# Five small reorderings in a hybrid mLSTM and windowed-attention layer: softmax negation, factor stores, key tanhs, side stores, and the loads of a scan

## The chip, the cores and the metric

The kernel runs on one core of a Trainium2 chip. The metric is the device time of one execution in microseconds, and the median of several runs is compared. A core has a tensor engine (PE), a vector engine (VectorE, DVE in the profile), a scalar engine (ScalarE, ACT), GpSimd (POOL) and SyncE (SP), which here does nothing but issue DMAs. Each engine takes its own list of instructions in order. Tiles move between HBM and SBUF by DMA; PE writes to PSUM banks, which VectorE and ScalarE empty.

## The reference

One layer over a sequence of 4096 rows of width 1024. A norm and an input projection give the columns of two groups of heads. Group A is a matrix memory (mLSTM), scanned in 32 chunks of 128 rows, once in each direction:

```
qk_a = jax.nn.silu(centred_depthwise_conv(qk_a, conv_w, conv_b))
h = sigmoid(o_a) * (h_fwd + h_bwd)
y_a = rms(h) * mhn_w * silu(z_a)
```

In each chunk the scan has scores of q and k times a decay matrix E, a part from the carried state C times the weighted q (W), a division by the larger of two denominators, and the update of the state. Group B is attention in a window of 128 rows to either side, with 8 query heads of 64 on 2 key heads, a position bias and a sink logit:

```
m = jnp.maximum(jnp.max(scores, axis=-1), sink_l)
p = jnp.exp(scores - m[..., None])
denom = jnp.sum(p, axis=-1) + jnp.exp(sink_l - m)
```

Both outputs are concatenated and go through an output projection; the input is added, and a last norm ends it. All of it is fp32, and matrices are split into a high and a low part so that three products give fp32 accuracy.

## The kernel before, in words

Four stages follow one another. `pass1` (L161) reads x in 16 blocks of 256 rows, norms and transposes it, projects queries, keys and values of group B and does the attention. `pass2` (L876) goes backwards over 8 blocks of 512 rows, makes q, k and v of group A with the convolution, and carries the backward state. `pass3` (L1411) does the scans of both directions in 32 chunks, and beside them a stream of gate projections (`gate_stream`, L1268) with seven products P0 to P6 in place of eight for each pair of chunks. `tail` is the output projection and the last norm.

The order of PE's work is written out by hand: `interleave` and `place` set pieces of one kind of work between units of another at given fractions. The instructions of the other engines are put in order by a scheduler, from the order in which the program issues them and their dependences; `behind(c, ins)` says that what is issued inside it may stand no earlier than `ins`, and `high_priority` draws PSUM evictions ahead. Tiles come from pools that are used in turn: a load into a tile waits until the last reader of the buffer's former tile is done. Two of them matter here: `xtile` (14 buffers of 4 KB per partition, for E, W, CC, the raw rows r and the operands op) and `slot` (2 KB tiles, for hs, z, o and others).

*Attention.* A slot is a key head of a chunk of 128 queries, 64 in all. `att_a` (L361) does a slot's scores in four groups g: two matmuls into `sp` (L379), then one VectorE instruction (L382) that adds the bias, writes the negated scores `s` and leaves their minimum with the negated sink in a column of `NG`. After the fourth group come four exponentials on ACT (L390), each of which uses one column of `NG`, so that each may run as soon as its own column is there. `att_t` transposes (L410; copies to `pt`, L412 on ACT and L413 on VectorE), `att_o` multiplies by v (L424; evictions to `ab`, L436 and L437) and stores `at_d` (L439). In slot sl the scores are those of slot sl+2.

*The last attention stretch* (from about 500 us) has 16 pieces `w2_piece`, each of which loads a part of the value weights (`w2s`, L575) and scales and splits it (L696 on ACT, L697 on VectorE). `keep_first` (L612) stores the norm factors of the first rows, six DMAs of 128 single words to `rs_d` (L615), and is the piece hooked in at place 8.

*pass2.* `qkproj(b, m)` makes one projection of 512 columns of block b: 24 matmuls `up` (L1031), the copy U (L1035), the convolution of one ACT step (L1048) and four VectorE steps (L1050), and then `finish` (L1052): tanh on ACT (L1054), a product on VectorE (L1055), a store. m 0 to 3 are queries, 4 to 7 keys; the tanh of m = 7, and in all blocks but the last also of 0 and 3, is put off by `c.late`. `ktp` (L1092) transposes a key head and splits it to `kt` (L1098, L1099), `kvmm` (L1115) updates the state C (L1134) and stores `kf_d` (L1140). `side(b)` (L983) fits in loads, sums and stores that prepare the gate products.

*pass3.* `load_scan` (L1241) issues the loads of a chunk by name: q, k, kf, v, CC (the backward state) and, in two broadcast halves each, E and W. In chunk n the loop at L1537 loads CC, E and W of chunk n+2, makes the forward state (`state`, L1453) of chunk n+1 with kf, and loads kf of n+2; then its pieces among 42 matmuls of the gate stream: `decays` of n+1 (masks of E on POOL, L1437, exponentials on ACT, L1441), four `heads` (L1465), the load of v for n+2 with `weigh_q` (L1459, W times q) of n+1, `yout` (L1508, transposes `yp` and a store) of n−1, `scores` (L1444, S and its product with E) of n+1, and last `FIN` (L1503: hs times its norm times z; the norm's power is done on POOL, L1499). In the gate stream `ahead(i)` (L1342), which is called four matmuls into product i, splits the operand of product i+1 (ACT copy L1288, subtraction L1289 on VectorE or POOL) and issues the loads that a small plan lists: whole operands 5 and 6 and the next pair's 0, and raw rows 3 and 2. `evict` (L1310) empties a product with additions to o and z.

## Time and profile before

| what | value |
|---|---|
| median of 3 runs | 2195.59 us (2193.04 to 2196.16) |
| the profiled execution | 2192.97 us, of which its span is 2191.2 us |
| PE busy | 2126.5 us, 97% |
| VectorE, ACT, POOL busy | 1544.2, 1139.0, 710.6 us |
| granted clock of PE | 0.997 |
| HBM read, written | 305.20 MB, 153.17 MB |

Durations and waits are those of the one profiled execution. A row of the trace in order of time has the start in us from the span's start, the time in us, the engine, the line, the operation, the tiles (out<-in), the shape, a count where neighbours are merged, and in brackets how long the engine had stood idle and what released it. SPq is SyncE's queue of DMA issues. A row of waits has the total in us, how many times, and the longest. The stages lie at about 0 to 600 us (`pass1`), 600 to 1200 (`pass2`), 1200 to 1715 (`pass3`) and from there to the end (`tail`).

### The profile page before, as it was taken

To read this page: it belongs to the slowest core of one execution; us is meant where nothing else is said; L and a number is where in the kernel's file an instruction comes from. 1 tells how busy PE (TensorE), PEld (TensorE's weight loads), DVE (VectorE), ACT (ScalarE), POOL (GpSimd) and SP (SyncE) were. 2 spreads that over 40 slices of the span, in tenths; PEclk is the share of its full clock that TensorE was granted. 3 is DMA by queue.
4 is the path that set the end of the run, shared out by engine and by line. 5 is a ranking of instruction groups with operands and counts; after the bars stand their busy time and mean duration, and the time that the engine had idled before them with its cause. 6 is when DMAs were issued, how large, how long until landed. Compare 5 with 4: busy or idle time off the path is not lost.

```text
span 2191.2 us, 35245 instructions
## 1 busy us (share of the span) xinstructions
PE 2126.5 (97%) x12034; PEld 1839.1 (84%) x12034; DVE 1544.2 (70%) x3195; ACT 1139.0 (52%) x2764; POOL 710.6 (32%) x1049
## 2 busy tenths in 40 slices
PE   8999999998999999999999999999999999999998
PEld 7999999998898787888887888888887788888886
DVE  6677777777877777677647777776667543877776
ACT  7788888876653444444434554555455321333323
POOL 3576665651013333332311322323222111112222
PEclk9999999999999999999999999999999999999999
DMA  7665654543236745654586988777878998667765
GB/s 255 188 207 149 186 190 139 185 133 82 71 118 228 238 160 170 236 188 132 170 274 239 305 278 264 247 242 258 271 252 291 334 355 286 184 186 185 192 191 146
DMA packets 286433, 460.72 MB, mean 210 GB/s; under 512 B 23851, under 2 KB 151851, under 8 KB 284716
## 3 DMA queue, kind: packets, MB, share of 16 engines
q1 hardware_dynamic: 246880, 323.94, 45.2%
q0 software_dynamic: 39136, 134.25, 20.5%
q8 instruction: 95, 1.56, 0.3%
q14 instruction: 86, 0.70, 0.1%
q10 hardware_dynamic: 236, 0.27, 0.0%
HBM read 305.20 MB, written 153.17 MB: 209 GB/s over the span
## 4 chain that ended last, share of the span: by engine, by line
PE 60%; DMA 14%; DVE 10%; issue 7%; ACT 5%; POOL 3%; SPq 1%; POOLq 0%; ACTq 0%; DVEq 0%
PE up L1031 13%; PE qp L547 8%; PE P L1337 6%; PE v2p L1004 6%; DMA xr<-x 5%; PE op L424 3%; PE tp L410 3%; DMA E<-m_d 3%; PE sp L379 3%; PE zbp L151 3%; PE zbp L153 3%; PE zbp L152 3%; DMA xb<-xT_d 2%; DMA W<-w_d 2%; PE num L1474 1%
## 5 line engine op out<-in xcount | busy, mean ns | idle before, releaser
L1337 PE MATMUL P<-wt,op 128*128 128x512 f32 x1344 | 365.7, 407 | 14.0 <-DVE z L1325 11.6
L1031 PE MATMUL up<-xb,w 128*128 128x512 f32 x1344 | 334.7, 396 | 0.0
L1685 PE MATMUL o<-wo,yo 128*128 128x512 f32 (+1 forms) x1356 | 312.3, 392 | 0.0
L1685 PEld LDWEIGHTS o<-wo,yo 128*128 128x128 f32 x1356 | 253.3, 188 | 59.0
L1337 PEld LDWEIGHTS P<-wt,op 128*128 128x128 f32 x1344 | 237.5, 189 | 62.0 <-DVE z L1325 15.4
L1031 PEld LDWEIGHTS up<-xb,w 128*128 128x128 f32 x1344 | 245.0, 188 | 48.8
L1050 DVE SCALAR_TENSOR_TENSOR qk<-U,cw,qk 128x512 f32<-128x512 f32 x256 | 197.3, 771 | 85.3 <-ACT qk L1048 73.5
L547 PE MATMUL qp<-xT,wqb 128*128 128x256 f32 x1536 | 242.6, 288 | 0.1
L547 PEld LDWEIGHTS qp<-xT,wqb 128*128 128x128 f32 x1536 | 214.4, 190 | 8.5 <-DVE wqb L320 0.5
L413 DVE TENSOR_TENSOR pt<-tp,pt 128x512 fp32r<-128x512 f32 x188 | 129.6, 690 | 68.6 <-ACT pt L412 66.7
L390 ACT ACTIVATE s<-s,NG 128x320 f32<-128x320 f32 (+1 forms) x256 | 142.3, 557 | 50.8 <-DVE NG L382 49.3
L382 DVE CUSTOM_DVE_ANT_0 s<-sp,G,nsink 128x320 f32<-128x320 f32 (+1 forms) x256 | 138.0, 539 | 38.6 <-PE sp L379 36.7
L1004 PE MATMUL v2p<-w,xb 128*128 128x512 f32 x672 | 158.3, 395 | 2.9 <-DMA xb<-xT_d 2.2
L1004 PEld LDWEIGHTS v2p<-w,xb 128*128 128x128 f32 x672 | 125.8, 188 | 34.1 <-DMA xb<-xT_d 3.5
L412 ACT CAST pt<-tp 128x512 fp32r<-128x512 f32 x188 | 109.9, 584 | 46.7 <-PE tp L410 21.7
L424 PE MATMUL op<-pt,v 128*128 128x512 f32 x376 | 122.0, 406 | 10.2 <-DVE ab L437 9.4
L1488 ACT ACTIVATE hs<-num,r 128x128 f32<-128x128 f32 x128 | 46.9, 366 | 157.2 <-DVE r L1485 90.6
L379 PE MATMUL sp<-kk,q 128*128 128x320 f32 (+2 forms) x512 | 119.5, 314 | 3.2 <-DVE NG L382 2.2
L410 PE MATMUL tp<-ident,s 128*128 128x128 f32 x752 | 113.0, 272 | 0.2 <-DVE pt L413 0.2
L151 PE MATMUL zbp<-xc,w 128*128 128x512 f32 x256 | 102.4, 400 | 2.6 <-DVE az L1400 1.4
L1503 DVE SCALAR_TENSOR_TENSOR hs<-hs,ss,z 128x128 f32<-128x128 f32 x128 | 46.5, 424 | 79.8 <-POOL ss L1499 79.8
L1054 ACT ACTIVATE th<-qk 128x512 f32<-128x512 f32 x64 | 40.5, 632 | 116.6 <-DVE qk L1050 116.6
(306 smaller groups left out, 4641.0 us busy)
## 6 DMA issues: line engine op xcount, KB each, us to landing
xc<-xT_d SPq DMA_DIRECT2D x64, 512.0 KB, 7.5
xT_d<-xT POOLq DMA_DIRECT2D x52, 512.0 KB, 6.4
xb<-xT_d SPq DMA_DIRECT2D x48, 514.0 KB, 8.6
op<-xT_d SPq DMA_DIRECT2D x96, 256.0 KB, 5.3
E<-m_d SPq DMA_DIRECT2D x64, 256.0 KB, 6.4
W<-w_d SPq DMA_DIRECT2D x64, 256.0 KB, 6.8
y<-y_d SPq DMA_DIRECT2D x32, 512.0 KB, 3.5
out<-xr POOLq DMA_DIRECT2D x31, 512.0 KB, 6.1
```

The costliest lines, as they stand in the source:

```text
L151: nc.tensor.matmul(out, wl, xh, start=first, stop=False)
L379: nc.tensor.matmul(sp[:, lo:hi], qt, kk[:, kv, z, col - 128 + lo:col - 128 + hi], start=(z == 0), stop=(z == 1))
L382: nc.vector.tensor_tensor_reduce(out=s[:, lo:hi], in0=sp[:, lo:hi], in1=bias[0][:, kv * 2 + m, lo - 64 * half:hi - 64 * half], op0=ALU.add ...
L390: LAST["act"] = nc.scalar.activation(ps[g][:, kept(g)], ps[g][:, kept(g)], AF.Exp, scale=-1.0, bias=ng[:, g:g + 1], accum_out=rs[:, g:g + 1])
L410: nc.tensor.transpose(tp[:, g * 128:(g + 1) * 128], ps[g][:, j * 128:(j + 1) * 128], c.ident)
L424: nc.tensor.matmul(op, vt, pt[:, z, :], start=(i == 0 and z == 0), stop=(i == len(js) - 1 and z == 1))
L547: nc.tensor.matmul(qp, wq[k // 2][:, k % 2, w, m * 128:m * 128 + 128], x[k], start=(k == 0 and j == 0), stop=(k == KT - 1 and j == 2))
L1004: nc.tensor.matmul(vp, a, wv[k // 2][:, k % 2, m, :], start=(k == 0 and j == 0), stop=(k == KT - 1 and j == 2))
L1031: nc.tensor.matmul(up[:, 0:hi - lo], w[k // 2][:, k % 2, a, cs], x, start=(k == 0 and j == 0), stop=(k == KT - 1 and j == 2))
L1050: nc.vector.scalar_tensor_tensor(acc, U[:, t:t + 512], cw[:, cm, t:t + 1], acc, ALU.mult, ALU.add)
L1337: nc.tensor.matmul(P[i], OPS[j, i][:, k, z, :], c.wt[i][k][m], start=k == 0 and a == 0, stop=k == 3 and a == 2)
L1685: nc.tensor.matmul(p, a[:, z, k, :], w[k // 2][:, k % 2, m, lo:hi], start=k == 0 and z == 1, stop=k == 3 and z == 0 and m == 0)
```

## The change

Five edits, all in the order of instructions but for the first:

1. *Softmax.* The VectorE instruction of a group now keeps the scores with their sign and leaves their maximum in a column of a new tile `st`; after the fourth group one further VectorE instruction on 128×4 elements negates the four maxima and takes the minimum with the negated sink, into `NG`. The four exponentials read `NG` and so all come behind it.
2. *Factor stores.* `keep_first` is hooked in at place 94 in place of 8, behind the last `w2_piece`.
3. *Key tanhs.* The tanh and product of all key projections m = 4 to 7 are put off; those of 4, 5 and 6 are issued behind the convolution of the projection that follows.
4. *Side stores.* What `side` issues from the second list stands behind the latest store of `kf_d`.
5. *Scans.* W and CC are loaded for chunk n+1 in chunk n (before: n+2); `state(n)` makes the state of n+1 in chunk n, behind the product of the scores with E; v is loaded at the piece before the third head and for n+1, kf of n+2 with the piece that had v; the operands 5, 6 and the next 0 are loaded one product later; `weigh_q(0)` goes behind the first product with E.

The diff:

```diff
@@ att_a
-                ST[sl] = ([], list(range(jl // 128, jr // 128)))
-            ps, _ = ST[sl]
+                st = wk.tile([128, 4], F32, tag="st", bufs=4, name=f"st{sl}")
+                ST[sl] = ([], list(range(jl // 128, jr // 128)), st)
+            ps, _, mx = ST[sl]
...
-                                           op0=ALU.add, op1=ALU.min, scale=-1.0,
-                                           scalar=nsink[:, kv, half, m:m + 1], accum_out=ng[:, g:g + 1])
+                                           op0=ALU.add, op1=ALU.max, scale=1.0, scalar=-3e38,
+                                           accum_out=mx[:, g:g + 1])
             ps.append(s)
             if g < 3:
                 return
+            nc.vector.scalar_tensor_tensor(ng, mx, -1.0, nsink[:, kv].rearrange("p h m -> p (h m)"), ALU.mult, ALU.min)
             for g in range(4):
-                LAST["act"] = nc.scalar.activation(ps[g][:, kept(g)], ps[g][:, kept(g)], AF.Exp, scale=-1.0,
-                                                   bias=ng[:, g:g + 1], accum_out=rs[:, g:g + 1])
+                LAST["act"] = nc.scalar.activation(ps[g][:, kept(g)], ps[g][:, kept(g)], AF.Exp, bias=ng[:, g:g + 1],
+                                                   accum_out=rs[:, g:g + 1])
@@ pass1
-        hooks.append((8, keep_first))
+        hooks.append((94, keep_first))
@@ side
-                        f()
+                        with behind(c, c.kfs):
+                            f()
@@ qkproj
-                if m == 7 or m in (0, 3) and b:
+                if m > 3 or m in (0, 3) and b:
                     c.late[m] = finish
@@ kvmm
-                nc.gpsimd.dma_start(c.kf_d[n], kf.rearrange("p h d -> p (h d)"))
+                c.kfs = nc.gpsimd.dma_start(c.kf_d[n], kf.rearrange("p h d -> p (h d)"))
@@ pass2, after the units of projection m
+                if m > 4:
+                    c.late[m - 1]()
@@ ahead
-            plan = [(2, whole, j, 5), (3, whole, j, 6), (4, whole, j + 1, 0), (4, raw, j + 1, 3), (5, raw, j + 1, 2)]
+            plan = [(3, whole, j, 5), (4, whole, j, 6), (5, whole, j + 1, 0), (4, raw, j + 1, 3), (5, raw, j + 1, 2)]
             if j == 0:
-                plan = [(3, whole, 0, 5), (4, whole, 1, 0), (4, raw, 1, 3), (5, raw, 1, 2)]
+                plan = plan[:1] + plan[2:]
@@ pass3
         decays(0)
-        weigh_q(0)
...
         with behind(c, c.em):
-            state(0)
+            weigh_q(0)
             weigh_q(1)
...
             m = n + 1
+            if n:
+                load(m, ("w", "cc"))
+            if m < NCH:
+                with behind(c, c.em):
+                    state(n)
             with behind(c, c.rawd if n == 0 else None):
-                load(n + 2, ("cc", "e", "w"))
+                load(n + 2, ("e",))
                 if n == 0:
                     load(2, ("q",))
-            if n + 2 < NCH:
-                state(m)
-            with behind(c, c.rawd if n == 0 else None):
-                load(n + 2, ("kf",))
...
-            pieces.append(lambda: (load(n + 2, ("v",)), weigh_q(m) if m > 1 else None))
+            pieces.insert(4, lambda: load(m, ("v",)) if n else None)
+            pieces.append(lambda: (load(n + 2, ("kf",)), weigh_q(m) if m > 1 else None))
```

The rows below are places in an engine's order, with the program's names (a row has the line, the operation, out<-in and the shape; the last number of a name only tells instances apart). The lines of the changed kernel are two to six higher.

SyncE's order in the last attention stretch, where w2s00 to w2s07 and w2s10 to w2s17 are the sixteen parts of the value weights, at_d the attention's stores and v_d those of the values. Before:

```order
L575 DMA w2s01_6768<-w_in 128x512
L439 DMA at_d_70<-ab25_6710 128x512
L575 DMA w2s02_6830<-w_in 128x512
L615 DMA rs_d_79<-rstd0_0_164 128x1
L615 DMA rs_d_79<-rstd0_1_171 128x1
L615 DMA rs_d_79<-rstd1_292 128x1 x2
L615 DMA rs_d_79<-rstd2_521 128x1 x2
L575 DMA w2s03_6907<-w_in 128x512
```

and now:

```order
L577 DMA w2s16_7765<-w_in 128x512
L577 DMA w2s17_7807<-w_in 128x512
L606 DMA v_d_77<-v2t31_7607 128x516
L441 DMA at_d_70<-ab29_7739 128x512
L617 DMA rs_d_79<-rstd0_0_164 128x1
L617 DMA rs_d_79<-rstd0_1_171 128x1
L617 DMA rs_d_79<-rstd1_292 128x1 x2
L617 DMA rs_d_79<-rstd2_521 128x1 x2
L606 DMA v_d_77<-v2t29_7839 128x516
L441 DMA at_d_70<-ab30_7910 128x512
```

The six stores of rs_d stood between the parts w2s02 and w2s03 and now stand behind the last part, between two stores of the attention.

VectorE's order in block 6 of `pass2`, where qk6_7 is the fourth key projection and qk6_0 the one issued next, th the tanh, kt the transposed keys and C27 a state. Before:

```order
L1099 TENSOR_TENSOR kt6_1_1_9113<-ktp6_1_9107,kt6_1_0_9112 128x512
L1050 SCALAR_TENSOR_TENSOR qk6_7_9067<-U6_7_9038,cw_7335,qk6_7_9067 128x512 x2
L1055 SCALAR_TENSOR_TENSOR qk6_7_9067<-th6_7_9117,qk6_7_9067 128x512
L1134 SCALAR_TENSOR_TENSOR C27_9166<-C28_8652,decay_8180,kv27_0_9168 128x129
L1050 SCALAR_TENSOR_TENSOR qk6_0_9131<-U6_0_9080,cw_7335,qk6_0_9131 128x512
L1099 TENSOR_TENSOR kt6_2_1_9149<-ktp6_2_9143,kt6_2_0_9148 128x512
L1134 SCALAR_TENSOR_TENSOR C27_9166<-C28_8652,decay_8180,kv27_1_9177 128x129
```

and now:

```order
L1053 SCALAR_TENSOR_TENSOR qk6_7_9191<-U6_7_9162,cw_7445,qk6_7_9191 128x512 x2
L1102 TENSOR_TENSOR kt6_1_1_9241<-ktp6_1_9235,kt6_1_0_9240 128x512
L1058 SCALAR_TENSOR_TENSOR qk6_7_9191<-th6_7_9245,qk6_7_9191 128x512
L1053 SCALAR_TENSOR_TENSOR qk6_0_9259<-U6_0_9208,cw_7445,qk6_0_9259 128x512
L1102 TENSOR_TENSOR kt6_2_1_9277<-ktp6_2_9271,kt6_2_0_9276 128x512
L1053 SCALAR_TENSOR_TENSOR qk6_0_9259<-U6_0_9208,cw_7445,qk6_0_9259 128x512
L1137 SCALAR_TENSOR_TENSOR C27_9294<-C28_8780,decay_8304,kv27_0_9296 128x129
L1053 SCALAR_TENSOR_TENSOR qk6_0_9259<-U6_0_9208,cw_7445,qk6_0_9259 128x512
L1137 SCALAR_TENSOR_TENSOR C27_9294<-C28_8780,decay_8304,kv27_1_9305 128x129
```

The product with the tanh (L1055) came right behind the last steps of qk6_7, and now (L1058) the subtraction kt6_1_1 stands between them; kt6_2_1 stood behind the first update of C27 and now stands ahead of both. On ACT, the copy U and the first convolution step of the projections 5 to 7 now stand ahead of the tanh of the projection before.

SyncE's order in `pass3` for one pair of chunks: r are raw rows, op the operands of the gate products (op8_5 is the one of product 5 of pair 8), and the others the loads of a scan by chunk. Before:

```order
L1256 DMA lkf16_15914<-kf_d_76 128x516
L1234 DMA op8_5_16021<-xT_d_69 128x4x128 x2
L1256 DMA lv16_16012<-v_d_77 128x516
L1234 DMA op8_6_16065<-xT_d_69 128x4x128 x2
L1260 DMA CC17_16070<-cb_d_78 128x4x129
L1265 DMA E17_16072<-m_d_72 128x512
L1256 DMA lq17_16046<-q_d_74 128x512
L1265 DMA E17_16072<-m_d_72 128x512
L1256 DMA lk16_16044<-k_d_75 128x512
L1265 DMA W17_16075<-w_d_73 128x512 x2
L1256 DMA lkf17_16082<-kf_d_76 128x516
```

and now, for the next pair:

```order
L1270 DMA W17_16351<-w_d_73 128x512 x2
L1265 DMA CC17_16354<-cb_d_78 128x4x129
L1270 DMA E18_16360<-m_d_72 128x512
L1261 DMA lkf17_16304<-kf_d_76 128x516
L1270 DMA E18_16360<-m_d_72 128x512
L1261 DMA lq18_16335<-q_d_74 128x512
L1261 DMA lk17_16333<-k_d_75 128x512
L1239 DMA op9_5_16511<-xT_d_69 128x4x128 x2
L1261 DMA lv17_16417<-v_d_77 128x516
L1270 DMA W18_16516<-w_d_73 128x512 x2
L1265 DMA CC18_16519<-cb_d_78 128x4x129
L1270 DMA E19_16525<-m_d_72 128x512
```

E of a chunk now comes right behind W and CC of the chunk before it, W is loaded a chunk later than E, and op_5 stands ahead of one v and W in place of two chunks' loads.

VectorE's order from the product of the scores with E16 to hs15, where op9_4 is the subtraction that reads r9_3 last. Before:

```order
L1451 TENSOR_TENSOR E16_15904<-S16_16208,E16_15904 128x512 x2
L1489 SCALAR_TENSOR_TENSOR hs15_16131<-num15_2_16144,r15_1_16163,hs15_16131 128x128
L1493 SCALAR_TENSOR_TENSOR hs15_16131<-o15_15676,hs15_16131 128x512
L1328 TENSOR_TENSOR o17_16008<-P8_6_16204,o17_16008 128x512
L1289 TENSOR_TENSOR op9_2_16303<-r9_2_16181,op9_2_16303 128x4x128
L1463 TENSOR_TENSOR W18_16239<-W18_16239,lq18_16217 128x1024
L1498 TENSOR_SCALAR ss3_15_16172<-ss3_15_16172 128x4
L1503 SCALAR_TENSOR_TENSOR hs15_16131<-hs15_16131,ss3_15_16172,z15_15772 128x128 x4
```

and now:

```order
L1494 SCALAR_TENSOR_TENSOR hs15_16242<-num15_2_16266,r15_1_16283,hs15_16242 128x128
L1456 TENSOR_TENSOR E16_16028<-S16_16326,E16_16028 128x512
L1461 SCALAR_TENSOR_TENSOR CC17_16354<-CC16_16187,decay_8304,lkf16_16130 128x129 x4
L1294 TENSOR_TENSOR op9_4_16508<-r9_3_16235,op9_4_16508 128x4x128
L1498 SCALAR_TENSOR_TENSOR hs15_16242<-o15_15793,hs15_16242 128x512
L1333 TENSOR_TENSOR o17_16125<-P8_6_16321,o17_16125 128x512
L1503 TENSOR_SCALAR ss3_15_16292<-ss3_15_16292 128x4
L1488 SCALAR_TENSOR_TENSOR r16_0_16402<-num16_0_16388,TM_8490 128x4
L1489 TENSOR_TENSOR r16_0_16402<-r16_0_16402,num16_0_16388 128x4
L1490 RECIPROCAL r16_0_16402<-r16_0_16402 128x4
L1468 TENSOR_TENSOR W18_16516<-W18_16516,lq18_16335 128x1024
L1508 SCALAR_TENSOR_TENSOR hs15_16242<-hs15_16242,ss3_15_16292,z15_15884 128x128 x4
```

The subtraction op9_4 came behind hs15 and now stands ahead of it, the updates CC17 stand between the product with E16 and op9_4, and W18 stands ahead of hs15 in both.

More of the change, by code (lines that the diff above doesn't have):

```diff
@@ L403, in att_t @@
         def att_t(sl, i):
-            ps, js = ST[sl]
+            ps, js, _ = ST[sl]
             if i >= len(js):
```

## The prediction

> **What bounds the kernel now.** I read the page first, then TensorE's (PE's) waits by cause, then busy time by stage, and only then the instructions in order of time around the largest waits. The page's busy line and the costliest group:
>
> ```profile
> PE 2126.5 (97%) x12034; PEld 1839.1 (84%) x12034; DVE 1544.2 (70%) x3195; ACT 1139.0 (52%) x2764; POOL 710.6 (32%) x1049
> L1337 PE MATMUL P<-wt,op 128*128 128x512 f32 x1344 | 365.7, 407 | 14.0 <-DVE z L1325 11.6
> ```
>
> PE is busy 2126.5 of 2191.2 us. The change adds or removes no matmul, so nothing it does can be worth more than the 64.7 us in which PE stands still. Which of these it can reach is told by the waits of PE (total, times, longest):
>
> ```profile
> PE P L1337 <- DVE z L1325: 11.6, 12, 1.9
> PE op L424 <- DVE ab L437: 9.4, 10, 3.0
> PE ktp L1096 <- DVE kt L1099: 7.7, 5, 2.1
> PE sp L379 <- DVE NG L382: 2.2, 1, 2.2
> PE S L1449 <- DVE o L1328: 1.6, 1, 1.6
> ```
>
> and by the busy time of PE in stages (first time after the comma is PE; then PEld, DVE, ACT, POOL, clock, DMA share, GB/s):
>
> ```profile
> 100.00:500.00 400.00, 395.78 (x2986) 380.94 (x2985) 310.74 (x764) 323.62 (x844) 255.48 (x327) 1.00 0.55 168
> 500.00:600.00 100.00, 93.60 (x601) 84.13 (x600) 77.43 (x191) 67.31 (x167) 5.34 (x18) 0.97 0.25 67
> 1225.00:1700.00 475.00, 459.11 (x2661) 392.89 (x2660) 342.53 (x878) 251.34 (x784) 133.68 (x151) 1.00 0.81 264
> ```
>
> So attention's steady part leaves 4.2 us, its last stretch 6.4, the scans 15.9. Each edit touches one of these places. The clock is 0.97 to 1.00 in all of them and plays no part.
>
> **Factor stores.** SP's queue, and what stood behind it on ACT and PE:
>
> ```profile
> 506.24 2.81 SPq L615 DMA_DIRECT2D rs_d<-rstd  x6
> 509.15 12.46 SPq L575 DMA_DIRECT2D w2s<-w_in  x3
> DMA to landing us min/median/max: 2.7/2.9/9.4
> 519.76 1.37 ACT L696 ACTIVATE w<-w2s,nw 128x512 fp32r<-128x512 f32 x2 [5.21 <-DMA w2s<-w_in]
> 521.91 0.56 PE L379 MATMUL sp<-kk,q 128*128 128x320 f32 x2 [2.19 <-DVE NG L382]
> 526.86 1.22 PE L424 MATMUL op<-pt,v 128*128 128x512 f32 x2 [1.36 <-DVE ab L437]
> ```
>
> The third row is for the loads of w2s: 2.9 us as a rule, 9.4 at worst, and the worst is the one issued straight behind the six stores of single words. ACT takes its instructions in order, so it sat 5.21 us before the multiplication of that piece with softmax exponentials and PSUM copies queued behind it, and PE ran dry twice: 2.19 + 1.36 = 3.6 us. With the stores behind the last of the sixteen w2s loads nothing is queued behind them that PE waits for soon. I take −3.6, with ends −6.4 (all that PE idles from 500 to 600) and 0 (another load is late in its place).
>
> **Key tanhs.** Block 6, where the key projection's tanh is last:
>
> ```profile
> 718.97 0.63 ACT L1054 ACTIVATE th<-qk 128x512 f32<-128x512 f32 x1 [3.22 <-DVE qk L1050]
> 721.71 0.68 DVE L1099 TENSOR_TENSOR kt<-ktp,kt 128x512 fp32r<-128x512 f32 x1
> 722.54 0.63 PE L1096 MATMUL ktp<-ident,qk 128*128 128x128 f32 x4 [2.05 <-DVE kt L1099]
> ACT th L1054 <- DVE qk L1050: 116.6, 49, 3.3
> ```
>
> ACT reaches the tanh before the convolution's last VectorE step and stands 3.22 us; the next projection's copy U and the cast of kt stand behind it, VectorE gets its subtraction for kt at 721.71, and ktp6_3, which needs the PSUM bank that this subtraction reads, starts 2.05 us late. The wait on the tanh is paid 49 times, but only five of them reach PE, 7.7 us in all. In the new order ACT copies and begins the next projection ahead of the tanh of the one before, so VectorE goes from one projection to the next without that wait and comes to kt6_2_1 sooner, which also stands ahead of both updates of C27. The tanh of the last projection itself keeps its place on ACT, and its wait may stay. No instruction is added. Two of the five lie in block 0 (the largest at 1200.09, below), with other work around them than in block 6:
>
> ```profile
> 1200.09 0.63 PE L1096 MATMUL ktp<-ident,qk 128*128 128x128 f32 x4 [2.02 <-DVE kt L1099]
> ```
>
> Of these two I count half, so −6, with ends −7.7 and 0. The side stores that now follow kf_d on POOL delay writes that are read many tens of microseconds later: 0.
>
> **Scans.** A pair of chunks, in order of time:
>
> ```profile
> 1523.98 0.51 SPq L1265 DMA_DIRECT2D W<-w_d  x1
> 1524.59 0.43 SPq L1256 DMA_DIRECT2D lkf<-kf_d  x1
> 1533.60 1.21 SPq L1234 DMA_DIRECT2D op<-xT_d  x2
> 1537.49 0.56 SPq L1265 DMA_DIRECT2D E<-m_d  x1
> 1538.92 0.47 SPq L1265 DMA_DIRECT2D E<-m_d  x1
> 1543.65 0.64 POOL L1437 TENSOR_SCALAR_AFFINE_SELECT E<-E 128x512 f32<-128x512 f32 x1 [6.33 <-DMA E<-m_d]
> 1546.71 0.64 POOL L1437 TENSOR_SCALAR_AFFINE_SELECT E<-E 128x512 f32<-128x512 f32 x1 [2.42 <-DMA E<-m_d]
> 1548.39 1.14 DVE L1503 SCALAR_TENSOR_TENSOR hs<-hs,ss,z 128x128 f32<-128x128 f32 x4 [6.37 <-POOL ss L1499]
> 1552.06 0.96 PE L1337 MATMUL P<-wt,op 128*128 128x512 f32 x3 [1.91 <-DVE z L1325]
> SPq L1234 <- POOL op L1289: 71.5, 13, 6.3
> ```
>
> SP issues nothing from 1524.6 to 1533.6: its next load (op) waits for a buffer that a subtraction still reads, once in each of 13 pairs. Then the loads come in a burst; E, issued at 1537.49 and 1538.92, lands after 6.2 and 7.8 us, POOL's mask waits, the power behind it on POOL too, VectorE sits 6.37 us before hs with W and the addition to z behind it, and PE loses 1.91. This chain is the 11.6 us of the first wait above. In the new order the E loads of a chunk go out a chunk ahead of their use with W and state behind them, and op_5 no longer stands ahead of them; the chain goes: −11.6.
>
> What is late next is W. It is now loaded in the chunk in which it is multiplied. The load of W18 takes the buffer of r9_3, whose last reader is the subtraction op9_4, and in the new VectorE order that stands behind the product of E16 and four CC updates. The rows for this:
>
> ```profile
> 1458.97 1.05 PE L1449 MATMUL S<-lq,lk 128*128 128x128 f32 x8
> 1472.26 0.60 PE L1512 MATMUL yp<-ident,hs 128*128 128x128 f32 x4
> 1528.83 1.23 DVE L1463 TENSOR_TENSOR W<-W,lq 128x1024 f32<-128x1024 f32 x1 [0.92 <-DMA W<-w_d]
> 1538.08 1.28 DVE L1451 TENSOR_TENSOR E<-S,E 128x512 f32<-128x512 f32 x2
> L1456 DVE SCALAR_TENSOR_TENSOR CC<-CC,decay,lkf 128x129 f32<-128x129 f32 x116 | 34.5, 340 | 0.0
> L1289 DVE TENSOR_TENSOR op<-r,op 128x512 fp32r<-128x512 f32 x30 | 23.9, 798 | 0.0
> DMA to landing us min/median/max: 4.6/6.8/8.3
> ```
>
> From the scores S16 (1458.97) PE needs 13.3 us to yp15 (1472.26), which wants hs15, and VectorE does W18 just ahead of hs15. The chain from S16: some 2.3 us to the end of the scores and VectorE's turn (an estimate: E's product in another chunk, at 1538.08, comes 2.3 us behind S at 1535.76), 1.28 for E, 4 × 0.34 for CC, 0.8 for op9_4: 5.7. Two issues of W follow, half a microsecond apart: 6.2. Landing: the last row, for loads of W, gives 4.6 to 8.3; the one issued at 1523.98, after a pause of SP's, was used at 1528.83, 4.85 later. Then W 1.22 and hs 1.14. Ends: 6.2 + 4.6 + 2.4 = 13.2, nothing late; with 6.8, 15.4, late by 2.1. SP pauses ahead of W18, so I take the row of 4.85 and 0.25 more for two op loads in front: late by 0.4 us in some 14 pairs, +5.6. The scans come to −11.6 + 5.6 = −6, ends −15.9 and +18 (14 × 2.1 − 11.6). The first W, which held up PE 1.6 us before the first scores (the row S above), is now multiplied behind them: −1.6.
>
> The Trainium skill speaks against this edit: its page "DMA: Bandwidth & Descriptors" (Rules for kernel authors) has a DMA issued early and waited for late. Before the change the queue broke that rule for E and kept it for W; after it, the other way round. The trace agrees as far as E's lateness goes; what W's would do is the second rival.
>
> **Softmax.** The negation becomes one VectorE instruction per slot, 64 of 128×4; the trace of before has that shape on L1483, and the exponentials that now wait for it:
>
> ```profile
> L1483 DVE SCALAR_TENSOR_TENSOR r<-num,TM x64: 131/151/163, 1224.4 to 1701.7; 128x4 f32<-128x4 f32 x64
> L390 ACT ACTIVATE s<-s,NG 128x320 f32<-128x320 f32 (+1 forms) x256 | 142.3, 557 | 50.8 <-DVE NG L382 49.3
> ```
>
> 64 × 0.151 = 9.7 us of VectorE. It is busy 310.7 of 400 us between 100 and 500, so the work fits beside PE's; and scores are made two slots ahead of their transposes. The first three of four exponentials can no longer start singly, and a run of 4 × 0.557 = 2.2 us on ACT can hold up a PSUM copy. PE's waits for ab there are small; I take +1.5, ends 0 and 9.7. A gain is excluded: nothing is taken from any engine. By the Trainium skill, page "Perfetto Trace Analysis" (Optimizing Scalar/DVE Operations), a VectorE instruction costs about 60 ns fixed when it works on SBUF, which would make the upper end an estimated 3.8 us; the measured row is taken.
>
> **Sum.** −3.6 − 6 − 6 − 1.6 + 1.5 = −15.7 from the profiled execution of 2192.97 us: 2177.3. That execution lay 2.6 us under the median of its three runs (2195.59), which is the likelier base: 2195.6 − 15.7 = 2179.9.
>
> **Rivals.**
> *Something else is late in the scans.* E is early, yet PE goes on waiting, for o or z behind a fuller VectorE: the scans give 0 and the rest −9.7, so 2186. For it: ACT and VectorE trade in every chunk. Against: the idle 6.37 us on VectorE shows spare time. Chance 0.17.
> *W becomes the wait (slower).* If loads of W land as they did as a rule, 6.8 us, hs15 is late by 2.1 in 14 pairs, +29.4 against −11.6 and the other edits' −9.7: +8, 2204. It decides from about 1.5 us late per pair (14 × 1.5 = 21 = 11.6 + 9.7), a landing of 6.2, and from 1.8, a landing of 6.5, the loss can be told from no change. For it: DMA is busy 0.81 in this stage. Against: the burst that made the 6.8 is what the change breaks up. This is what the skill's rule on early issue would give. Chance 0.16.
> *Softmax's instructions show.* If all 9.7 us reach PE: −17.2 + 9.7 = −7.5, 2188. For it: ACT is busy 323.6 of 400 us there. Against: two slots of lead. Chance 0.10.
> *The waits only move.* Each late row has a neighbour nearly as late, and the sum is 0: 2195.6. Against: the chains above each have one cause that the order removes. Chance 0.05.
> *As forecast:* 0.52, with its own range 2170 to 2187.
>
> **How the numbers follow.** A measurement of this kernel tells about 0.2%, 4.4 us, from no change, so faster means under 2191.2 and slower over 2200. Faster: 0.52, and most of the first and third rival, 0.21: 0.73. Slower: the second rival, 0.16. The rest, 0.11, the same. The range goes from all gains at their ends (−6.4 − 7.7 − 15.9 − 1.6 = −31.6: 2164) to just under the second rival's time: 2164 to 2203.
>
> **What would show it.** Right: no idle of ACT at L696 over 1 us; the ktp wait under 2 us in total; POOL's idle before E's mask near nothing, the P←z wait under 3 us, and the window 1225 to 1700 with under 10 us of PE idle. Wrong: a wait of yp on hs with VectorE idle before W for its DMA (second rival); a P wait on o or z of the old size (first); PE idle between 100 and 500 above 8 us (third). If PE's idle in the last attention stretch stays near 6.4 us the stores were not the cause.

## The result

The changed kernel takes 2173.94 us (median of four runs, 2170.39 to 2177.91) against 2194.86 us before (four runs, 2193.04 to 2196.16): a ratio of 0.9906, with a 95% interval of 0.9887 to 0.9925. That is 20.9 us less, where 15.7 were forecast. The span of the profiled execution is 2168.7 us against 2191.2.

The sum came out nearly right, but three of its terms did not. The page's busy line, the group of the gate products, and PE's longest waits after the change, without one of 6.5 us in `pass1` that was there before (6.6):

```profile
PE 2116.4 (98%) x12034; PEld 1834.4 (85%) x12034; DVE 1547.1 (71%) x3259; ACT 1132.2 (52%) x2764; POOL 704.2 (32%) x1049
L1342 PE MATMUL P<-wt,op 128*128 128x512 f32 x1344 | 360.4, 406 | 0.4 <-DMA op<-xT_d 0.4
```

```profile
PE tp L412 <- DVE pt L415: 15.6, 13, 1.8
PE op L426 <- DVE ab L439: 7.0, 6, 2.4
PE v2p L1007 <- DMA xb<-xT_d: 3.1, 2, 2.1
PE ktp L1099 <- DVE kt L1102: 2.8, 2, 1.5
```

The waits of P on z, 11.6 us in 12 places, are gone; of the waits of ktp on kt only the two in block 0 are left; and a new one has come that was not there before, of the attention's transposes tp on pt, 15.6 us in 13 places. By stage (the first number after the comma is PE's busy time):

```profile
100.00:500.00 400.00, 385.72 (x2916) 371.51 (x2916) 311.53 (x786) 310.38 (x826) 250.24 (x316) 1.00 0.46 164
500.00:600.00 100.00, 93.41 (x623) 83.91 (x621) 80.82 (x214) 70.43 (x184) 10.14 (x28) 1.00 0.25 81
1225.00:1700.00 475.00, 472.79 (x2741) 408.13 (x2740) 346.58 (x898) 259.05 (x798) 130.53 (x156) 1.00 0.87 280
```

In the scans PE idles 2.2 us in place of 15.9; in the steady part of attention 14.3 in place of 4.2.

Idle time is a blunt measure here: the four transposes yp of a row shown further down count as 0.98 us busy where they wait for their input, and as 0.60 in the row of the prediction. It is safer to take the start of the same instruction in both traces. So measured, from the first product of query block 3 to that of block 13, from the first `up` of `pass2` to the first gate product, and from the first scores to the last gate product:

| stage | before, us | changed, us | difference |
|---|---|---|---|
| `pass1`, ten blocks of queries | 341.2 | 353.1 | +11.9 |
| `pass1`, from there to the last `op` | 141.6 | 138.0 | −3.6 |
| `pass2` | 583.5 | 577.1 | −6.3 |
| first gate product to first scores | 30.4 | 28.3 | −2.0 |
| scans | 462.6 | 444.5 | −18.2 |

Ahead of these stages the first product of query block 3 starts at 115.1 us in place of 118.5, and the time behind the last gate product is 1.0 us shorter; with the table that makes up the 22.5 us between the two spans. The same table for the experiments is at the end of the next section.

### The profile page after: what moved, and what is told of

The parts are those of the page before. It is cut to its first block, busy times and chain, and to the rows that moved or that the text cites. A ratio compares the mean times of both kernels' runs of the same rounds, so it can differ in the third digit from the quotient of the medians.

```text
span 2168.7 us, 35317 instructions
## 1 busy us (share of the span) xinstructions
PE 2116.4 (98%) x12034; PEld 1834.4 (85%) x12034; DVE 1547.1 (71%) x3259; ACT 1132.2 (52%) x2764; POOL 704.2 (32%) x1049
## 5 line engine op out<-in xcount | busy, mean ns | idle before, releaser
L1342 PE MATMUL P<-wt,op 128*128 128x512 f32 x1344 | 360.4, 406 | 0.4 <-DMA op<-xT_d 0.4
L383 DVE CUSTOM_DVE_ANT_0 s<-sp,G 128x320 f32<-128x320 f32 (+1 forms) x256 | 122.3, 478 | 27.8 <-PE sp L380 25.8
L412 PE MATMUL tp<-ident,s 128*128 128x128 f32 x752 | 113.5, 273 | 15.9 <-DVE pt L415 15.6
L151 PE MATMUL zbp<-xc,w 128*128 128x512 f32 x256 | 102.2, 399 | 1.9 <-DVE az L1405 1.4
L412 PEld LDWEIGHTS tp<-ident,s 128*128 128x128 f32 x752 | 85.5, 140 | 20.8 <-issue 17.7
L153 PE MATMUL zbp<-xc,w 128*128 128x512 f32 x256 | 101.0, 395 | 0.0
```

The lines of the kernel that those rows point to most:

```text
L383: nc.vector.tensor_tensor_reduce(out=s[:, lo:hi], in0=sp[:, lo:hi], in1=bias[0][:, kv * 2 + m, lo - 64 * half:hi - 64 * half], op0=ALU.add ...
L412: nc.tensor.transpose(tp[:, g * 128:(g + 1) * 128], ps[g][:, j * 128:(j + 1) * 128], c.ident)
L1342: nc.tensor.matmul(P[i], OPS[j, i][:, k, z, :], c.wt[i][k][m], start=k == 0 and a == 0, stop=k == 3 and a == 2)
```

## The experiments

All were timed beside the kernel before on the same chip. Its own median lay between 2189.6 and 2198.0 us from one group of runs to another, so the ratios are compared and not the medians.

**The parts, one at a time.** The changed kernel without its softmax edit (the three edited places of `att_a` and `att_t` put back):

> The changed kernel with the old softmax, everything else as changed. Theory (the separate negation costs PE once per block of pass 1, about 1.3 us in each of some ten): the blocks between 115 and 468 us take 34.0 us again in place of 35.3, the waits of tp on pt are gone, and the time is about 12 us under the changed kernel's 2174: 2162. Rival (pass 1 is slower because the stores moved and shifted the pieces between PE's units, not because of the softmax): the blocks stay at 35.3 us and the time at 2174.

0.9866 (0.9844 to 0.9888). The ten blocks took 340.9 us again. So the softmax edit cost nearly a third of what the other four gained.

The kernel before with the softmax edit alone:

> The kernel before with only the separate negation. Theory: pass 1 grows by some 12 us and nothing else moves: 2207, slower by 0.5%, with PE waiting for pt once per block. Rival (the cost is no more than the 64 small instructions off PE's path, +1.5 as I forecast): 2196, no change.

1.0047 (1.0031 to 1.0063), 10.3 us slower; the ten blocks took 352.5 us, with the same wait:

```profile
PE tp L412 <- DVE pt L415: 18.6, 15, 2.2
```

Ahead of the blocks the edit gains: query block 3 starts at 115.1 us here and in the changed kernel, and at 118.0 to 119.2 in the kernels with the old softmax.

The kernel before with the scans' edits alone:

> The kernel before with only the scans' edits (loads, state, v, kf, the plan of operands, the first W). Theory (the scans' gain is their own): from the first scores to the last product 18 us less, the first scores 2 us earlier, 2175. Rival (part of it came from pass 1 or 2 handing over buffers in another state): under 12 us, 2183 or more. By the sum of my prediction it would be 7.6 us, 2187.

0.9935 (0.9910 to 0.9959), 14 us less; the scans took 448.9 us in place of 462.6.

The kernel before with the key tanhs and the side stores:

```diff
-                if m == 7 or m in (0, 3) and b:
+                if m > 3 or m in (0, 3) and b:
...
+                if m > 4:
+                    c.late[m - 1]()
...
+                        with behind(c, c.kfs):
+                            f()
```

> The kernel before with only the late key tanhs and the side stores behind kf_d. Theory: pass 2 is 6 us shorter, from the waits of ktp on kt in blocks 6 to 4, 2189. Rival (the 6 us of pass 2 came from the shift that the other edits gave the side loads): 2 us or less, 2193.

0.9956 (0.9943 to 0.9969), 9.6 us less, more than either expected; `pass2` took 574.0 us. What the side stores have in it was not tried apart. ACT's wait of the tanhs, 116.6 us in 49 places before, is halved:

```profile
  DVE qk L1051: 58.6, 32
```

The kernel before with the factor stores alone (place 8 to 94):

> The kernel before with only the factor stores behind the last part of the value weights. Theory: the waits at 522 to 527 us go and nothing comes in their place, 3.5 us less. Rival (the store of the attention's output ahead of the six small stores is as late as the weights' load was, and holds up the buffer ab): no change.

0.9972 (0.9958 to 0.9987), 6.1 us less, with the 3.5 that were expected inside the interval (2.9 to 9.2), and the stretch to the last `op` took 134.8 us in place of 141.6.

**Why the scans gain.** The loads without the plan of operands, and the plan without the loads:

```diff
-            plan = [(2, whole, j, 5), (3, whole, j, 6), (4, whole, j + 1, 0), (4, raw, j + 1, 3), (5, raw, j + 1, 2)]
+            plan = [(3, whole, j, 5), (4, whole, j, 6), (5, whole, j + 1, 0), (4, raw, j + 1, 3), (5, raw, j + 1, 2)]
```

> The kernel before with the scans' loads, states, v and kf as changed and the first W behind the first product, but the plan of the operands 5, 6 and 0 as before. My reading (E goes out early because W and state are a chunk later): nearly all of the scans' gain, 14 of 16 us. Rival (SyncE's wait at operand 5, which the plan puts one product later, is the cause of the late E): 4 us or less of gain.

> The kernel before with only the plan of the operands 5, 6 and the next 0 one product later. Theory after the run of the loads alone (SyncE's wait at operand 5 is what makes E late): E lands in time, the waits of P on z go, 10 to 16 us less than before. Rival (plan and loads are each useless alone, since E is taken from a queue that both fill): 4 us or less.

The loads alone gave 0.9986 (0.9973 to 1.0000), the plan alone 1.0002 (0.9989 to 1.0014). Neither my reading nor the rival that I had put against it in the first run holds: the gain needs both, as the rival in the second run said. With the plan alone SyncE waits at the operand for other readers, and POOL waits for E as before, 108.9 us in 38 places against 98.3 in 38 (SyncE's waits, PE's waits, and POOL's at one pair):

```profile
SPq L1234 <- PE num L1474: 114.5, 15, 8.8
```

```profile
PE P L1337 <- DVE r L1484: 13.1, 13, 1.7
```

```profile
1546.12 0.63 POOL L1437 TENSOR_SCALAR_AFFINE_SELECT E<-E 128x512 f32<-128x512 f32 x1 [5.63 <-DMA E<-m_d]
```

With the loads alone E comes sooner (POOL waits 33.4 us for it, in 20 places), but now W stands behind operand 5 and its wait, and VectorE sits before W:

```profile
1511.80 1.23 DVE L1463 TENSOR_TENSOR W<-W,lq 128x1024 f32<-128x1024 f32 x1 [4.56 <-DMA W<-w_d]
```

With both edits POOL waits for E no less than before; the first row below is its total. What has gone is what stood behind that wait: VectorE's products hs waited 79.8 us in 31 places for the power ss on POOL, and in the changed kernel 4.3 in 5. Before, the power came behind both masks of E in the pair that the prediction shows, at 1547.31 behind 1546.71. In a pair of the changed kernel it comes ahead of them:

```profile
POOL E L1442 <- DMA E<-m_d: 112.9, 30, 7.2
1456.95 1.04 POOL L1504 TENSOR_TENSOR ss<-ss,nhalf 128x4 f32<-128x4 f32 x1 [4.45 <-DVE r L1488]
1463.60 0.64 POOL L1442 TENSOR_SCALAR_AFFINE_SELECT E<-E 128x512 f32<-128x512 f32 x1 [5.61 <-DMA E<-m_d]
```

To see how near its limit W is with both, the changed kernel with the old softmax and W and CC issued behind the E of the next chunk:

```diff
-            if n:
-                load(m, ("w", "cc"))
-            if m < NCH:
-                with behind(c, c.em):
-                    state(n)
             with behind(c, c.rawd if n == 0 else None):
                 load(n + 2, ("e",))
                 if n == 0:
                     load(2, ("q",))
+            if n:
+                load(m, ("w", "cc"))
+            if m < NCH:
+                with behind(c, c.em):
+                    state(n)
```

> The changed kernel with the old softmax, and with W and CC of a chunk issued behind E of the next one in place of ahead of it, about 1 us later. If W is at its limit (in the changed kernel the last product with hs ends within 0.6 us of PE's need in every second chunk), PE waits about 1 us more at yp in some 14 pairs: 2172 against 2160.6. Rival (VectorE has room and W is not on the path): 2161, no change.

0.9929 (0.9902 to 0.9956) against 0.9866 without that swap: about 14 us of the gain went, and the scans took 461.7 us, as before any change. The loss has the size that I expected, but not for the reason: PE waits on another tile of VectorE's than I named, o and not hs:

```profile
PE P L1340 <- DVE o L1331: 10.8, 12, 1.9
```

Nor does VectorE wait more for W: 15.3 us in 11 places, against 33.1 in 20 without the swap. In one of these places, VectorE's W and its subtraction for an operand run beside two of the same subtractions on GpSimd (POOL), and o comes behind them:

```profile
1512.10 2.10 DVE L1466 TENSOR_TENSOR W<-W,lq 128x1024 f32<-128x1024 f32 x1 [0.67 <-DMA W<-w_d]
1514.19 1.70 DVE L1292 TENSOR_TENSOR op<-r,op 128x512 fp32r<-128x512 f32 x1
1511.82 3.52 POOL L1292 TENSOR_TENSOR op<-r,op 128x512 fp32r<-128x512 f32 x2
1516.61 1.89 PE L1340 MATMUL P<-wt,op 128*128 128x512 f32 x7 [0.60 <-DVE o L1331]
```

W took 1.23 us and the subtraction 0.8 in the rows of the prediction. Of the 30 subtractions on VectorE 12 are stretched so, 11.9 us beyond the median together, against 8 and 3.2 us without the swap. So one position in the queue decides here, but that W is at its limit is not shown by it.

**Why the softmax costs.** My first reading was that four exponentials and the norm's two squares in a row on ACT come ahead of the cast pt. The negation in two halves, and then the squares held back behind the third cast:

```diff
-            if g < 3:
+            if g % 2 == 0:
                 return
-            nc.vector.scalar_tensor_tensor(ng, mx, -1.0, nsink[:, kv].rearrange("p h m -> p (h m)"), ALU.mult, ALU.min)
-            for g in range(4):
+            nc.vector.scalar_tensor_tensor(ng[:, g - 1:g + 1], mx[:, g - 1:g + 1], -1.0, nsink[:, kv, half, :],
+                                           ALU.mult, ALU.min)
+            for g in (g - 1, g):
```

> The changed kernel with the negation done twice per slot, on two groups each, so 128 small VectorE instructions in place of 64, and two exponentials may start after the second group. Bunching theory (PE waits because four exponentials and the norm's two squares come in one run on ACT ahead of the cast pt that empties a PSUM bank): with only two exponentials ahead of the squares most of the 11 to 12 us of pass 1 go, blocks near 34.1 us, total near 2163. Rival (the small instructions themselves fill VectorE): blocks longer than 35.3 us, total 2174 to 2184.

```diff
-            nc.scalar.copy(pt[:, 0, :], tp)
+            LAST["pt"] = nc.scalar.copy(pt[:, 0, :], tp)
...
-            A1 = slot(4 * b) + [lambda: norm_rows(b + 4, LAST["act"])]
+            A1 = slot(4 * b) + [lambda: norm_rows(b + 4, LAST["pt"])]
```

> The changed kernel with the norm's two squares on ACT held back behind the third cast pt of the slot; the 64 negations and the four exponentials in a row stay. Bunching theory with the squares as the last straw: the wait of tp on pt once per block goes or falls under 0.3 us, total near 2163. Rival (four exponentials in a row are enough, or VectorE is): blocks stay near 35.3 us, total near 2174.

The halves gave 1.0105 (1.0087 to 1.0124): 43 us slower than the changed kernel, far beyond both expectations. The squares held back gave 0.9873 (0.9857 to 0.9889), and the ten blocks took 339.4 us. So the squares are part of the chain. In the changed kernel it reads as follows (the second square runs from 235.41 to 236.45), and it recurs once in each of the ten blocks, with a wait of 1.3 to 1.8 us:

```profile
231.38 0.56 ACT L392 ACTIVATE s<-s,NG 128x320 f32<-128x320 f32 x1 [2.20 <-DVE NG L390]
234.37 1.04 ACT L213 ACTIVATE jk<-xr 128x1024 bf16<-128x1024 f32 x1
236.57 1.07 ACT L414 CAST pt<-tp 128x512 fp32r<-128x512 f32 x2
238.03 0.63 PE L412 MATMUL tp<-ident,s 128*128 128x128 f32 x4 [1.41 <-DVE pt L415]
```

With the squares held back a new wait of op on ab has come ahead of the blocks, 8.8 us at 79.38, so that block 3 starts at 122.9 us; what brings it was not tried. And why should two small instructions in place of one cost 43 us? VectorE's row of one in the halves, and GpSimd's rows at that time:

```profile
230.84 2.68 DVE L390 SCALAR_TENSOR_TENSOR NG<-st,nsink 128x2 f32<-128x2 f32 x1
```

```profile
231.00 1.44 POOL L691 TENSOR_TENSOR xraw<-xraw 128x512 f32<-128x512 f32 x1
232.23 1.25 POOL L275 TENSOR_TENSOR xT<-xraw,xT 128x512 fp32r<-128x512 f32 x1
```

An instruction on two elements per partition took 2.68 us, across two of GpSimd's, and ended at 233.52, with the second of them (233.48). In the changed kernel it is the same: VectorE's row of one, GpSimd's at that time, and the row of the whole line, which shows that it is common there (min, median and max in ns):

```profile
230.34 1.00 DVE L390 SCALAR_TENSOR_TENSOR NG<-st,nsink 128x4 f32<-128x4 f32 x1
```

```profile
230.01 1.30 POOL L693 TENSOR_TENSOR xraw<-xraw 128x512 f32<-128x512 f32 x1
```

```profile
L390 DVE SCALAR_TENSOR_TENSOR NG<-st,nsink x64: 143/164/1839, 39.6 to 592.8; 128x4 f32<-128x4 f32 x64
```

Of the 64 negations 25 took more than 0.3 us, 32 us beyond the median together, and 24 of these ended within a few hundredths of a microsecond of the end of an instruction of GpSimd's: 12 with an elementwise one, as here (231.34 and 231.31), and 12 with the DMA issue that follows the one in which they began, as here:

```profile
249.11 1.78 DVE L390 SCALAR_TENSOR_TENSOR NG<-st,nsink 128x4 f32<-128x4 f32 x1
249.04 1.16 POOL L275 TENSOR_TENSOR xT<-xraw,xT 128x512 fp32r<-128x512 f32 x1
250.08 0.81 POOL L291 DMA_DIRECT2D xT_d<-xT  x1
```

None of the 39 short ones lies within an elementwise instruction of GpSimd's. The Trainium skill has a rule for this: by its page "SBUF — State Buffer" (Who interferes with whom) VectorE and GpSimd share a pair of SBUF ports under a lock, and a VectorE instruction with both inputs in SBUF contends with a GpSimd instruction that reads SBUF. The trace agrees as to where the waits begin, 24 of 25 within such an instruction; that 12 of them last through the DMA issue behind it (0.81 us above) is more than the rule says. The instructions that attention repeats in each slot on VectorE read one input from PSUM; the new one reads two tiles of SBUF.

The test is an instruction with one tile as input and the sink as a per-partition scalar, four of them in place of one, all four behind the fourth group, so that ACT's order hardly moves:

```diff
-            nc.vector.scalar_tensor_tensor(ng, mx, -1.0, nsink[:, kv].rearrange("p h m -> p (h m)"), ALU.mult, ALU.min)
+            with behind(c, red):
+                for g in range(4):
+                    nc.vector.tensor_scalar(ng[:, g:g + 1], mx[:, g:g + 1], -1.0, nsink[:, kv, g // 2, g % 2:g % 2 + 1],
+                                            ALU.mult, ALU.min)
```

> The changed kernel with the one negation of 128x4 elements per slot made by four VectorE instructions of 128x1 instead, which take the sink from a per-partition scalar and so read one tile, not two; all four behind the fourth group, so ACT's order stays as changed (three or four exponentials in a row, then the squares). Theory (25 of the 64 negations are stretched to 1 or 1.8 us because they read two tiles from SBUF and end only when GpSimd's instruction ends): no instruction on this line over 0.3 us, the waits of tp on pt in pass 1 go or halve, total 2162 to 2168, although there are 256 small instructions. Rival (four exponentials and the squares in a row are enough by themselves): blocks stay at 35.3 us, total 2174 or more.

0.9826 (0.9809 to 0.9844), the fastest of all, better than both kernels by over 17 us. There are 256 small instructions, and they take more of VectorE's time together than the 64 did, but none waits, though 61 of them lie within an elementwise instruction of GpSimd's:

```profile
L391 DVE TENSOR_SCALAR NG<-st,nsink x256: 193/204/216, 39.4 to 578.5; 128x1 f32<-128x1 f32 x128
```

The ten blocks took 342.5 us, with the exponentials and the squares still in one run on ACT. With the squares held back, on the other hand, 27 of the 64 negations are still stretched, and the blocks took 339.4. So the cost in the blocks needs both links, the stretch and the squares ahead of the cast; both remedies together were not tried. As a last run, each of the four behind its own group:

```diff
-            with behind(c, red):
-                for g in range(4):
-                    nc.vector.tensor_scalar(ng[:, g:g + 1], mx[:, g:g + 1], -1.0, nsink[:, kv, g // 2, g % 2:g % 2 + 1],
-                                            ALU.mult, ALU.min)
+            nc.vector.tensor_scalar(ng[:, g:g + 1], mx[:, g:g + 1], -1.0, nsink[:, kv, half, m:m + 1],
+                                    ALU.mult, ALU.min)
+            if g < 3:
+                return
```

> The kernel with four one-tile negations per slot, each now behind its own group, so that the exponentials may start one by one again and ACT has one of them ahead of the squares. Theory (the stretch was the whole cost; bunching alone costs nothing once it is gone): as the run with the four behind the last group, ratio 0.982 to 0.984. Rival (bunching costs its own few tenths per block): 2 to 4 us less, ratio 0.981.

0.9912 (0.9895 to 0.9928): both expectations missed. None of the 256 is stretched, but the ten blocks are back at 353.8 us, with another wait:

```profile
PE op L426 <- DVE ab L439: 16.5, 18, 1.7
```

Once in each block VectorE now has the first group of the next slot ahead of the addition to ab, and PE waits 0.9 us for the single bank of op. So an order without the stretch can be as dear: this one has a price of the same size, by another wait, and what exactly moves ab in it was not tried.

The stages of all runs, in us, as in the first table (blocks; to the last `op`; `pass2`; scans):

| kernel | ratio | blocks | to last op | pass2 | scans |
|---|---|---|---|---|---|
| before | 1 | 341.2 | 141.6 | 583.5 | 462.6 |
| changed | 0.9906 | 353.1 | 138.0 | 577.1 | 444.5 |
| all but softmax | 0.9866 | 340.9 | 136.1 | 578.0 | 445.2 |
| softmax only | 1.0047 | 352.5 | 140.0 | 584.7 | 461.7 |
| scans only | 0.9935 | 340.8 | 139.5 | 586.4 | 448.9 |
| keys only | 0.9956 | 340.8 | 139.4 | 574.0 | 459.3 |
| stores only | 0.9972 | 341.3 | 134.8 | 588.8 | 459.8 |
| loads only | 0.9986 | 341.6 | 142.2 | 590.8 | 458.8 |
| plan only | 1.0002 | 344.2 | 140.4 | 586.0 | 459.1 |
| W behind E | 0.9929 | 345.3 | 136.3 | 577.1 | 461.7 |
| negation in halves | 1.0105 | 390.8 | 140.8 | 575.9 | 444.9 |
| squares behind pt | 0.9873 | 339.4 | 140.7 | 578.6 | 443.8 |
| negation by scalars | 0.9826 | 342.5 | 134.1 | 578.0 | 444.5 |
| scalars by group | 0.9912 | 353.8 | 137.2 | 576.5 | 449.6 |

The kernels whose `pass2` is the old one take 583.5 to 590.8 us there, so a stage of one execution is good to some microseconds; the eight with the new one take 574.0 to 578.6. The four with the scans as they were take 459.3 to 462.6, and the kernel before is the longest of them.

## Why the prediction was right, and where it was not

*Factor stores: right.* Forecast −3.6, measured −6.1, with an interval that holds the forecast (2.9 to 9.2). The loads of w2s land in 6.1 us at worst now, where it was 9.4:

```profile
DMA to landing us min/median/max: 2.6/3.2/6.1
```

My condition for a failure, PE's idle time from 500 to 600 staying near 6.4 us, was met: it is 6.6 (100.00 less 93.41, in the table of stages above). It was the wrong sign to look at in the changed kernel, since other waits of PE fell into that window: 1.2 us for ab at 592.92, and 2.0 of the 2.4 that end at 600.37. In the run with the stores alone PE idles 3.6 us there. The first of the two comes from the stores' new place: the attention's store just ahead of them was late, and ACT's copy to the one buffer ab waited for it:

```profile
591.57 0.58 ACT L438 COPY ab<-op 64x512 f32<-64x512 f32 x1 [2.84 <-DMA at_d<-ab]
```

*Key tanhs: right in kind, too small.* Forecast −6, measured −9.6 (6.8 to 12.5). The three waits in blocks 6 to 4 went and the two in block 0 did not go, where I had counted half (2.8 us are left, in the row of ktp above, where my sign asked for under 2). The rest may lie in ACT's wait, halved, which I had not priced since it did not reach PE by the view of waits; this was not shown.

*Scans: right direction, wrong second term, and the first for another reason.* Forecast −6 of −11.6 + 5.6, or −7.6 with the first W; measured 14 us less alone, the first W included (9 to 20). PE's waits on z are gone as forecast, and with them most of VectorE's waits for the power ss. But E does not come in time for POOL: POOL's idle time before E's mask, which I had near nothing, is 112.9 us (98.3 before). What has changed is that the power does not stand behind a late mask any more, as the rows above show for one pair. And with the loads alone, where E does come sooner, nothing like this is gained. The +5.6 for a late W did not come. The working of W's path was close, though: in one pair of the changed kernel the scores start at 1448.71, and

```profile
1460.34 1.22 DVE L1468 TENSOR_TENSOR W<-W,lq 128x1024 f32<-128x1024 f32 x1 [3.08 <-DMA W<-w_d]
1461.48 1.13 DVE L1508 SCALAR_TENSOR_TENSOR hs<-hs,ss,z 128x128 f32<-128x128 f32 x4
```

```profile
1462.01 0.98 PE L1517 MATMUL yp<-ident,hs 128*128 128x128 f32 x4
```

PE comes to yp 13.3 us after the scores, and the last of four products with hs ends 13.9 us after (1462.61 − 1448.71), where I had 13.7 for all of them (6.2 + 4.85 + 0.25 + 2.4). What I missed is that yp is four transposes, one per head, each of which needs only its own quarter of hs: the first quarter is done at about 1461.8, in time. So W has little to spare in this pair and costs nothing. How much later it could come was not shown: with W behind E the loss came by o and not by hs. The second rival (W becomes the wait) did not come. And the first row of the argument, that SyncE's wait at operand 5 was the cause, was only half of it: without that wait removed the later loads give 0.14%, and without the later loads its removal gives nothing.

*Softmax: wrong.* Forecast +1.5, measured +10.3. The third rival had the size (9.7), and its sign came, 14.3 us of idle time between 100 and 500; but that the size fits is luck, since its reason was not the cause: not the sum of the small instructions' times but those that wait for GpSimd, which make the four exponentials late, together with the squares and the cast pt behind them on ACT and PE's transposes behind that. The row that I priced it by, L1483 at 0.151 us, has one input in PSUM and stands in a stage where GpSimd is busy 28% of the time (133.68 of 475 us); in attention it is busy 64% (255.48 of 400). The step that failed is the sentence that the work fits beside PE's: a duration was carried from one stage to another without asking what else the instruction needs. The Trainium skill's 60 ns, at an upper end of 3.8 us, would have been further off still. That "nothing is taken from any engine" was wrong as well, to the other side. The add with a constant in place of the sink is faster; its groups on the page, before and after:

```profile
L382 DVE CUSTOM_DVE_ANT_0 s<-sp,G,nsink 128x320 f32<-128x320 f32 (+1 forms) x256 | 138.0, 539 | 38.6 <-PE sp L379 36.7
```

```profile
L383 DVE CUSTOM_DVE_ANT_0 s<-sp,G 128x320 f32<-128x320 f32 (+1 forms) x256 | 122.3, 478 | 27.8 <-PE sp L380 25.8
```

*First W: right in kind.* Forecast −1.6, measured −2.0 from the first gate product to the first scores, and the wait of S on o is gone. In the run with the scans' edits alone that wait is gone too, but the stretch took 30.1 us against 30.4, so the size is open.

The sum was closer than its terms: the gains came to 29.4 us (0.9866) where 17.2 were forecast, and the softmax took 8.8 of them back (0.9906 against 0.9866) where 1.5 were. The two errors, 12.2 and 7.3 us, have opposite signs, and that the total is only 5 us off is in part luck.

## What to carry to other kernels

Before a small VectorE instruction is priced by a row of its shape, look at where its inputs lie and at how busy GpSimd is in the stage where it will stand: with two tiles of SBUF as inputs it may wait out one or more GpSimd instructions, and a per-partition scalar in place of the second tile avoids that even at four times the count. The order that comes with it still has to be timed, as the last run shows. When several reorderings of one queue are made together, price the pair and not each alone, since the one may move the wait to where only the other removes it. And a wait on a tile that is used head by head ends when its first quarter is there.

## What the runs showed that was not expected

A VectorE instruction can be held through a whole run of GpSimd instructions that follow one another, not only until the end of the first: 2.68 us for two of them, above, and in the halves the longest is nearly five, from 498.90 to 503.80 across four (the last ends at 503.77):

```profile
L390 DVE SCALAR_TENSOR_TENSOR NG<-st,nsink x128: 99/161/4904, 37.4 to 642.1; 128x2 f32<-128x2 f32 x128
```

And a store that is issued ahead of six stores of single words can land as late as they do, 8.7 us after its issue: ACT's 2.84 us at 591.57 were for a store of the attention's that SyncE had issued just ahead of them:

```profile
582.84 0.33 SPq L441 DMA_DIRECT2D at_d<-ab  x1
583.21 3.91 SPq L617 DMA_DIRECT2D rs_d<-rstd  x6
```

It is not the rule: of the eight kernels with the stores in this place the same store took 8.7 us here, 9.8 with the squares held back, 4.0 with the negation by scalars, and 2.2 to 2.3 in the other five. What decides it was not tried.
